# A two-layer encoder on one core: the last MLP products turned to tokens on partitions, and the first products in a written order

## The chip, the cores and the metric

The kernel runs on one core of a Trainium2 chip. A core has TensorE (PE, matrix products), VectorE (DVE), ScalarE (ACT), GpSimd (POOL) and SyncE (SP, which here only starts transfers), each with an instruction stream of its own, and 16 DMA engines. The metric is the device time of one execution in microseconds (us). A weight load of TensorE (PEld in the profile) runs beside the products.

## The reference

A trunk of two layers over x, 512 tokens by 1024 features, float32:

```python
for i in range(2):
    g = sandwich_gains[i]
    h = rms_norm(x, g[0])
    m = parallel_conv_mla(h, ...) if i == 0 else conformer_conv(h, ...)
    x = x + rms_norm(m, g[1])
    h = rms_norm(x, g[2])
    x = x + rms_norm(square(relu(h @ w1[i])) @ w2[i], g[3])      # 1024 -> 4096 -> 1024
return x
```

`parallel_conv_mla` is one combined input projection (1024 to 2208 columns), a gated convolution of width 3 on one part, latent attention with 8 heads on the other, and one output projection. `conformer_conv` is a pointwise product to 2048 columns, a gate, a depthwise convolution of width 31 over the tokens, a LayerNorm, a swish and a second pointwise product. `rms_norm(v, g)` is v times the reciprocal root of its mean square over the 1024 features, times g.

## The kernel before

**Layout.** Everything lies with features on partitions: x is eight tiles of 128 features by 512 tokens. A weight strip is 128 x 1024 (512 KB). `strip` loads one through SP's queue into a raw buffer, ACT casts it to a high part (`whi`, L225), and POOL subtracts that from the raw one for a low part (`wlo`, L226), so that a product of float32 is three products of the shorter type that TensorE takes at full rate: high by high (L248), high by low (L249), low by high (L250). `linear` makes 8 x 3 of them for a strip, into one PSUM bank. Activations are split in the same way (`h`, `hid`): ACT makes the high copy (L232) and DVE the low one (L235).

**Halves.** The tokens are worked in two segments, A and B, of 256 and 256 in layer 0, and of 240 and 272 in layer 1 (A2, B2), since the convolution of half A needs 15 tokens to its right. A written list, M2, names the steps: `('up', 'A', 0, 1, 0, 8)` is half A, layer 0, group 1 of four hidden groups, strips 0 to 8; `down` is the second MLP product, `join` the norm and residual at the end of a sub-layer, `pw1` and `pw2` the pointwise products, `norm` the LayerNorm, `finish` the last norm and the stores. While the chain of one half runs (`join`, `norm`), `pace` and `hold` pull steps of the other half ahead, and `fill` deals out convolution taps between products. The last group of half B's last MLP and its `finish` stand in a list of their own, M3, with nothing beside them; `finish` there gives three of eight tiles to POOL (POOL_OUT) and their stores to ACT's queue.

**Norms.** A mean square is a sum over partitions: squares on ACT (L360), sums of tiles on DVE (L335), then TensorE with a vector of ones (L370) brings one number per token into a column for each 128 tokens. `rstd` (L391 to L428) makes the reciprocal root in some 13 small DVE operations. `spread` brings it back over all partitions by small products with an identity (L435). At the beginning, `R0` is this factor of the first norm, and the evacuations of the first projection's products (L613) multiply by it.

**The start.** `split_x` loads a tile of x, multiplies it by the gain on DVE (L577), and splits it; START lists in which order tiles and the first strips are asked for. Squares of x lag four tiles (LAG). No order is written there: a scheduler places the instructions of all engines by its own model of their times, as in the rest of the program, except for DVE in a part of M2.

Of the kernel before, what the change touches and what calls it, by code (L numbers as in the profile page):

```python
# [35 lines left out]
M2 = [('up', 'A', 0, 0, 0, 8), ('join', 'B', 0, 1), ('down', 'A', 0, 0, 0, 8), ('up', 'A', 0, 1, 0, 8), ('down', 'A', 0, 1, 0, 8), ('up', 'A', 0, 2, 0, 8), ('down', 'A', 0, 2, 0, 8), ('up', 'A', 0, 3, 0, 8), ('down', 'A', 0, 3, 0, 8), ('join', 'A', 0, 3), ('up', 'B', 0, 0, 0, 8), ('down', 'B', 0, 0, 0, 4), ('pw1', 'A', 0, 8), ('down', 'B', 0, 0, 4, 8), ('up', 'B', 0, 1, 0, 8), ('down', 'B', 0, 1, 0, 8), ('up', 'B', 0, 2, 0, 2), ('norm', 'A'), ('up', 'B', 0, 2, 2, 8), ('down', 'B', 0, 2, 0, 8), ('pw2', 'A', 0, 8), ('join', 'A', 1, 1), ('up', 'B', 0, 3, 0, 8), ('down', 'B', 0, 3, 0, 8), ('join', 'B', 0, 3), ('up', 'A', 1, 0, 0, 8), ('down', 'A', 1, 0, 0, 4), ('pw1', 'B', 0, 8), ('down', 'A', 1, 0, 4, 8), ('up', 'A', 1, 1, 0, 8), ('down', 'A', 1, 1, 0, 8), ('up', 'A', 1, 2, 0, 6), ('norm', 'B'), ('up', 'A', 1, 2, 6, 8), ('down', 'A', 1, 2, 0, 8), ('up', 'A', 1, 3, 0, 4), ('pw2', 'B', 0, 8), ('join', 'B', 1, 1), ('up', 'A', 1, 3, 4, 8), ('down', 'A', 1, 3, 0, 8), ('up', 'B', 1, 0, 0, 8), ('down', 'B', 1, 0, 0, 6), ('finish', 'A'), ('down', 'B', 1, 0, 6, 8), ('up', 'B', 1, 1, 0, 8), ('down', 'B', 1, 1, 0, 8), ('up', 'B', 1, 2, 0, 8), ('down', 'B', 1, 2, 0, 8)]  # L36
M3 = [('up', 'B', 1, 3, 0, 8), ('down', 'B', 1, 3, 0, 8), ('finish', 'B')]
# [53 lines left out]
class Seg:  # L91
# [23 lines left out]
HALVES = A, B = Seg(0, T // 2), Seg(T // 2, T)  # L115


A2, B2 = Seg(0, T // 2 - PAD), Seg(T // 2 - PAD, T, PAD)

STARTS = [0, 128, 256, 384, 112, 240, 368]  # L120
# [13 lines left out]
def trunk(ctx: ExitStack, tc: tile.TileContext, a, out: bass.AP):  # L134
# [32 lines left out]
    def accum():  # L167

        scope["turn"] += 1
        tags = [t for t in scope["acc"] if t != "pj" or not (convs or todo or scope.get("chain"))]  # L170
        return ps(tags[scope["turn"] % len(tags)])
# [14 lines left out]
    def ht(dt=F32):  # L186
        return new(ap, "h", 2 * NC, T + PAD, dt=dt)[:, :T]
# [4 lines left out]
    def hpair():  # L192
        return tuple(Win(new(ap, "h", 2 * NC, T + PAD, dt=F32R)) for _ in range(2))
# [6 lines left out]
    vec = cp.tile([P, NV], F32, name="vec")  # L200
    ident = kst[:, K_ID : K_ID + P]
# [70 lines left out]
    late, convs, todo, normed, credit, turn = [], [], [], [], [0.0], [0]  # L272
# [191 lines left out]
    def join(xs, ms, s, post, pre, hs, seg, h, mlp):  # L464
# [4 lines left out]
        hv = views(hs, seg)  # L469
# [101 lines left out]

    s0 = Sum(NC, FULL, nc.gpsimd if ADD0 else nc.vector, whole=W0)

    def split_x(j):
        load_x(xs[j], j)
        t, (hi, lo) = scratch(T), (h.t[:, :T] for h in hs[j])
        nc.vector.tensor_scalar(out=t, in0=xs[j].t, scalar1=col(gains(0, 0) + j), scalar2=None, op0=ALU.mult)  # L577
# [5 lines left out]
    win, j = [], 0  # L583
    for what in START:
        if what == "x":
            split_x(j)
            j += 1
        else:
            win.append(strip(a["win"][len(win)], cuts=what))
    nc.sync.dma_start(kst, a["consts"])  # L590
    nc.sync.dma_start(vec[:, V_QN:], a["vecs"][:, V_QN:])
    settle()
    for j in range(NC - LAG, NC):
        s0.square(xs[j].t)
        settle()
# [12 lines left out]
    def latent(m0, n, gain, slot):  # L608
        lat, ss = [], Sum(n, FULL, whole=WL)
        for j in range(n):  # L610
            acc = linear(win[m0 + j] if m0 + j < len(win) else strip(a["win"][m0 + j]), hs)
            t = tmp("ycat")
            nc.vector.tensor_tensor(out=t, in0=acc, in1=R0, op=ALU.mult)  # L613
# [338 lines left out]
    def finish_step(tok, h):  # L952
        seg = seg_of(h, 1)
        bc = rstds(sums[h], lack.pop(h))
        pool = POOL_OUT[h]
        if pool:
            bcs = tmp("t2")[:, : seg.w]
            nc.scalar.activation(bcs, bc, AF.Copy)

        def add(j, x, m):  # L960
            on_pool = j in pool
            eng = nc.gpsimd if on_pool else nc.vector
            eng.tensor_tensor(out=x, in0=x, in1=m, op=ALU.add)
            queue = nc.scalar if on_pool else nc.sync
            queue.dma_start(out[j * P : (j + 1) * P, seg.sl], x)

        for j in (*pool, *(j for j in range(NC) if j not in pool)):
            on_pool, x, m = j in pool, xs[j][seg.sl], ms[j][seg.sl]
            eng = nc.gpsimd if on_pool else nc.vector
            t = m if on_pool else scratch(seg.w)  # L970
            eng.tensor_tensor(out=t, in0=m, in1=bcs if on_pool else bc, op=ALU.mult)
            settle()
            late.append(lambda j=j, x=x, t=t: add(j, x, t))
            pace(2)
        settle()

    def run(program, in_order=True):
        for tok in program:
# [13 lines left out]
            elif what == "down":  # L992
                need(a["w2"][args[0], args[1], m] for m in range(c0, c1))
                for m in range(c0, c1):
                    add(down_step, h, *args, m)
            elif what == "wout":
# [4 lines left out]
            elif what == "attend":  # L1001
                add(lambda tok, h, half: attend(h, A if half == "A" else B), *args)
# [25 lines left out]
    nc.sync.dma_start(taps, a["taps"])  # L1028
    MLP = dict(acc=["S", "pj", "S", "pj", "S"], hid=("hid", 2 * NC, T), y=("y", 3, T))
# [56 lines left out]
def _pack(i):  # L1086
# [14 lines left out]
    for h in range(H):  # L1101
# [33 lines left out]
        "w2": np.stack([np.stack([_blocks(w2[n, g]) for g in range(4)]) for n in range(2)]),  # L1135
    }
# [18 lines left out]
```

## Time and profile before

| | |
|---|---|
| median of 3 runs | 1166.66 us (1165.98 to 1166.71) |
| the profiled execution | 1166.52 us |
| its span in the profile | 1164.6 us |
| mean granted TensorE clock | 0.996 of full |
| TensorE (PE) busy | 1132.3 us, 97% |
| POOL, ACT, DVE busy | 846.2, 663.8, 645.7 us |
| bytes moved by DMA | 183.99 MB, mean 158 GB/s |

A row of the timeline holds start and duration in us, the engine, the line of the kernel, the operation, output and inputs with their shapes, the number of records (x8) and, in brackets, how long the engine stood idle before and what released it. A row of a group holds the number of instructions, busy time in us, mean ns of one, and the idle time before them. A row of a stretch holds, after its limits: its length, then busy us and number of instructions for PE, PEld, DVE, ACT and POOL, the granted clock, the share of DMA time and GB/s. A product of 512 columns has rows of 0.39 us, which overlap: what counts is the step from one to the next. A row of L370 or L435 in float32 makes two records for each product.

### The profile page before, as it was taken

Reading aid. Unit: us, or ns where it says so; the run is one execution under the profiler, and the core shown is the slowest. Engines: PE = TensorE matmul, PEld = TensorE weight load, DVE = VectorE, ACT = ScalarE, POOL = GpSimd, SP = SyncE. Lnnn points to the kernel's source line nnn. Section 1 sums busy time; section 2 is a strip of 40 time slices with the busy share of each in tenths; the row PEclk is TensorE's granted clock in tenths of the full one; section 3 lists DMA queues with packets and bytes.
Section 4 is the critical chain, followed back from the end, with each engine's and each line's share of the span. In section 5 each row is a group of like instructions: output and inputs, shape, how many; then the busy total and the mean of one; then the engine's idle time right before and its main releaser. Section 6 shows DMA issues by size and latency. Waiting matters only on the chain.

```text
span 1164.6 us, 22863 instructions
## 1 busy us (share of the span) xinstructions
PE 1132.3 (97%) x8850; PEld 1093.1 (94%) x8850; DVE 645.7 (55%) x1696; ACT 663.8 (57%) x1221; POOL 846.2 (73%) x409
## 2 busy tenths in 40 slices
PE   7999989999999999999999999999999999999995
PEld 5788868999999999999999999999999999999995
DVE  5662699554522124499985265599985272322123
ACT  6531677466745457645566778546467685545352
POOL 5663563149988888598886978698887877887681
PEclk9999999999999999999999999999999999999998
DMA  6421332036656555366554555465655554653431
GB/s 209 156 85 30 101 106 73 1 116 231 205 179 198 182 180 187 126 219 195 178 188 161 182 181 191 151 212 192 198 182 181 173 174 161 213 179 123 150 131 39
DMA packets 55405, 183.99 MB, mean 158 GB/s; under 512 B 6401, under 2 KB 10881, under 8 KB 55297
## 3 DMA queue, kind: packets, MB, share of 16 engines
q1 hardware_dynamic: 54720, 181.86, 47.9%
q8 instruction: 69, 1.13, 0.4%
q10 hardware_dynamic: 576, 0.68, 0.2%
q14 instruction: 40, 0.32, 0.1%
HBM read 180.42 MB, written 2.10 MB: 157 GB/s over the span
## 4 chain that ended last, share of the span: by engine, by line
PE 92%; DVE 3%; ACT 3%; DMA 1%; issue 1%; POOL 0%; SPq 0%; POOLq 0%; ACTq 0%
PE S L248 23%; PE S L249 23%; PE S L250 22%; PE pj L248 7%; PE pj L249 7%; PE pj L250 7%; DVE pr L772 1%; PE mi L370 1%; PE mi L435 1%; ACT whi L225 1%; PE mi L775 1%; DVE s L766 1%; PE o L249 1%; PE o L250 0%; DVE pt L238 0%
## 5 line engine op out<-in xcount | busy, mean ns | idle before, releaser
L226 POOL TENSOR_TENSOR wlo<-raw,whi 128x1024 fp32r<-128x1024 f32 (+2 forms) x347 | 802.9, 2335 | 252.2 <-ACT whi L225 243.3
L225 ACT ACTIVATE whi<-raw 128x1024 fp32r<-128x1024 f32 (+2 forms) x347 | 355.7, 1031 | 378.0 <-PE S L249 176.6
L248 PE MATMUL S<-h,whi 128*128 128x256 f32 (+3 forms) x1216 | 346.8, 289 | 6.2 <-ACT h L232 3.4
L250 PE MATMUL S<-h,wlo 128*128 128x256 f32 (+3 forms) x1216 | 349.9, 289 | 0.0
L249 PE MATMUL S<-h,whi 128*128 128x256 f32 (+3 forms) x1216 | 349.8, 289 | 0.1
L248 PEld LDWEIGHTS S<-h,whi 128*128 128x128 f32 x1216 | 227.5, 189 | 12.2 <-ACT h L232 4.2
L249 PEld LDWEIGHTS S<-h,whi 128*128 128x128 f32 x1216 | 229.4, 189 | 4.3 <-DVE h L235 0.5
L250 PEld LDWEIGHTS S<-h,wlo 128*128 128x128 f32 x1216 | 229.5, 189 | 4.0 <-POOL wlo L226 0.3
L248 PE MATMUL S<-hid,whi 128*128 128x256 f32 (+2 forms) x824 | 230.3, 282 | 2.0 <-DVE acc L335 1.8
L249 PE MATMUL S<-hid,whi 128*128 128x256 f32 (+2 forms) x824 | 230.7, 281 | 0.0
L250 PE MATMUL S<-hid,wlo 128*128 128x256 f32 (+2 forms) x824 | 230.0, 280 | 0.0
L837 DVE SCALAR_TENSOR_TENSOR pj<-u,taps,pj 128x240 f32<-128x240 f32 (+1 forms) x464 | 192.4, 481 | 1.3
L248 PEld LDWEIGHTS S<-hid,whi 128*128 128x128 f32 x824 | 154.5, 189 | 2.8 <-DVE acc L335 2.2
L249 PEld LDWEIGHTS S<-hid,whi 128*128 128x128 f32 x824 | 155.4, 189 | 0.2 <-DVE hid L238 0.2
L250 PEld LDWEIGHTS S<-hid,wlo 128*128 128x128 f32 x824 | 155.4, 189 | 0.0
L248 PE MATMUL pj<-h,whi 128*128 128x272 f32 (+3 forms) x336 | 103.6, 308 | 6.9 <-ACT h L232 5.5
L249 PE MATMUL pj<-h,whi 128*128 128x272 f32 (+3 forms) x336 | 103.1, 307 | 0.0
L250 PE MATMUL pj<-h,wlo 128*128 128x272 f32 (+3 forms) x336 | 102.8, 306 | 0.0
L248 PEld LDWEIGHTS pj<-h,whi 128*128 128x128 f32 x336 | 63.7, 190 | 10.1 <-ACT h L232 5.8
L238 DVE TENSOR_TENSOR hid<-S,hid 128x256 fp32r<-128x256 f32 (+2 forms) x103 | 43.1, 419 | 51.2 <-ACT hid L232 50.9
L540 DVE TENSOR_TENSOR m<-S,m 128x256 f32<-128x256 f32 (+2 forms) x74 | 30.6, 416 | 65.3 <-PE S L250 65.3
L249 PEld LDWEIGHTS pj<-h,whi 128*128 128x128 f32 x336 | 63.6, 189 | 3.4 <-DVE h L235 0.9
(247 smaller groups left out, 1683.1 us busy)
## 6 DMA issues: line engine op xcount, KB each, us to landing
raw<-in_w SPq DMA_DIRECT2D x256, 512.0 KB, 3.4
raw<-in_pw SPq DMA_DIRECT2D x48, 512.0 KB, 3.4
raw<-in_win SPq DMA_DIRECT2D x16, 512.0 KB, 3.3
x<-in_xT SPq DMA_DIRECT2D x16, 256.0 KB, 4.2
raw<-in_wout SPq DMA_DIRECT2D x8, 512.0 KB, 3.3
raw<-in_wq SPq DMA_DIRECT2D x8, 192.0 KB, 2.4
out<-x SPq DMA_DIRECT2D x8, 120.0 KB, 2.6
out<-x SPq DMA_DIRECT2D x5, 136.0 KB, 1.7
```

Source lines behind the costliest of these rows:

```text
L225: nc.scalar.activation(h, r, AF.Copy)
L226: nc.gpsimd.tensor_tensor(out=lo[:, c0:c1], in0=r, in1=h.bitcast(F32), op=ALU.subtract)
L238: eng.tensor_tensor(out=lo, in0=src, in1=hi.bitcast(F32), op=ALU.subtract)
L248: nc.tensor.matmul(acc, sh, mh, start=i == 0, stop=False)
L249: nc.tensor.matmul(acc, sh, ml, start=False, stop=False)
L250: nc.tensor.matmul(acc, sl, mh, start=False, stop=i == n - 1)
L370: nc.tensor.matmul(s[:, b : b + 1], q[:, sl.start - self.seg.lo : sl.stop - self.seg.lo], one, start=i == 0, stop=i == len(self.parts) - 1,)
L435: nc.tensor.matmul(o[:, sl], r[:, b : b + 1].to_broadcast([bw, P]), ident[:bw, :bw], start=True, stop=True,)
L540: nc.vector.tensor_tensor(out=m[seg.sl], in0=acc, in1=m[seg.sl], op=ALU.add)
L766: nc.vector.reduce_max(out=mx, in_=S, axis=AX.X)
L772: eng.tensor_scalar(out=pr_, in0=pr_, scalar1=sm, scalar2=None, op0=ALU.mult)
L837: nc.vector.scalar_tensor_tensor(out=dst, in0=src, scalar=wk, in1=acc, op0=ALU.mult, op1=ALU.add)
```

## The change

It has four parts.

- **Segments.** Layer 0 is cut 272 and 240, layer 1 256 and 256. The shift of B2 and `views` go.
- **The last MLP of half B** (`turn`, `residual`, `end` in place of `down` and `finish`): the second products of layer 1 have tokens on partitions. A 128-token block of `hid` is the stationary side and a strip of a second copy of w2 (rows by all 1024 columns) the moving one, 512 columns wide, into four banks (two blocks by two column halves); groups are added up in SBUF. x of half B is turned by 16 transposes on TensorE (`residual_step`). In the last group, `end_step` makes block 0 for all strips, then block 1 in pieces of 512, 256 and 256 columns; each piece is added on DVE, squared on ACT with a sum along the row, and multiplied by the gain on POOL. The reciprocal root is then one number a partition, and the result leaves by DVE and two queues to a second output, `out_b`. M3 and POOL's part of `finish` go. `gtok` is that gain, one row spread over 128 partitions by a transfer on ACT's queue.
- **The start.** Under `manual_schedule` PE, DVE and ACT keep the order in which it is written: nine and three products of zeros (`busy`), and for each tile of x its scale, high copy and rest; the first two strips' products interleaved, tile by tile; then strip 2, and strip 3 around the spread of the first norm.
- **Kept.** The three lines that make `inv0` and `R0` after `spread_sb` are not in the diff, and stand behind the new block, which makes both tiles too.

```diff
-HALVES = A, B = Seg(0, T // 2), Seg(T // 2, T)
-A2, B2 = Seg(0, T // 2 - PAD), Seg(T // 2 - PAD, T, PAD)
+HALVES = A, B = Seg(0, T // 2 + PAD), Seg(T // 2 + PAD, T)
+A2, B2 = Seg(0, T // 2), Seg(T // 2, T)
...
-... ('up', 'B', 1, 0, 0, 8), ('down', 'B', 1, 0, 0, 6), ('finish', 'A'), ('down', 'B', 1, 0, 6, 8), ('up', 'B', 1, 1, 0, 8), ('down', 'B', 1, 1, 0, 8), ('up', 'B', 1, 2, 0, 8), ('down', 'B', 1, 2, 0, 8)]
-M3 = [('up', 'B', 1, 3, 0, 8), ('down', 'B', 1, 3, 0, 8), ('finish', 'B')]
+... ('up', 'B', 1, 0, 0, 8), ('turn', 'B', 1, 0, 0, 6), ('finish', 'A'), ('turn', 'B', 1, 0, 6, 8), ('up', 'B', 1, 1, 0, 8), ('residual', 'B'), ('turn', 'B', 1, 1, 0, 8), ('up', 'B', 1, 2, 0, 8), ('turn', 'B', 1, 2, 0, 8), ('up', 'B', 1, 3, 0, 8), ('end', 'B', 1, 3)]
...
-    def split_x(j):
-        load_x(xs[j], j)
-        t, (hi, lo) = scratch(T), (h.t[:, :T] for h in hs[j])
-        nc.vector.tensor_scalar(out=t, in0=xs[j].t, scalar1=col(gains(0, 0) + j), scalar2=None, op0=ALU.mult)
-        settle()
-        split((hi, lo), t, nc.vector, late=late)
-        if j >= LAG:
-            s0.square(xs[j - LAG].t)
...
+    with tc.manual_schedule(engines={E.PE, E.DVE, E.Activation}):
...
+        scale_x(0)
+        win.append(strip(a["win"][0], cuts=(128,)))
+        rest_x(0)
+        bit(0, 0)
+        busy(3)
+        scale_x(1)
+        win.append(strip(a["win"][1], cuts=(256, 512, 768)))
+        rest_x(1)
+        bit(0, 1)
+        bit(1, 0)
+        bit(1, 1)
+        for j in range(2, NC):
+            scale_x(j)
+            if j >= 4:
+                square_x(j - 4)
+            rest_x(j)
+            bit(0, j)
+            bit(1, j)
+        win.append(strip(a["win"][2]))
...
+        for j in range(1, NC):
+            if j + 3 < NC:
+                square_x(j + 3)
+            if j == 4:
+                win.append(strip(a["win"][3]))
+            last = add_x(j)
+        for k in range(NC):
+            bit(2, k)
+        win.append(strip(a["win"][4]))
+        s0 = Sum(NC, FULL)
+        s0.parts = [last]
+        root = rstd(s0.done(STARTS), D, inverse=inv0)[:, :NB]
+        for k in range(NC - 2):
+            bit(3, k)
+        nc.scalar.activation(R0, spread(root), AF.Copy)
+        for k in range(NC - 2, NC):
+            bit(3, k)
...
+    def turn_mm(acc, h, w, k, b, cols, n):
+        tok = slice(T // 2 + b * P, T // 2 + b * P + P)
+        x, c = hid[h][k], slice(cols.start + n, cols.stop + n)
+        return [
+            (acc[:, cols], x[0][tok], w[0][:, c], k == 0, False),
+            (acc[:, cols], x[0][tok], w[1][:, c], False, False),
+            (acc[:, cols], x[1][tok], w[0][:, c], False, k == NC - 1),
+        ]
...
+        for f in range(2):
+            piece(0, f, slice(0, T))
+        rest(0, slice(0, T))
+        r = root(0)
+        leave(0, r, 1)
+        piece(1, 0, slice(0, T))
+        for i in range(2):
+            cols = slice(i * T // 2, (i + 1) * T // 2)
+            rest(1, cols)
+            piece(1, 1, cols)
+        leave(1, root(1), 2)
...
+    nc.scalar.dma_start(gtok, a["gain"].to_broadcast([P, D]))
```

DVE at the start, before (L577 is the scale, L235 the subtraction for the low part):

```order
L577 TENSOR_SCALAR o_117<-x_80,vec 128x512
L235 TENSOR_TENSOR h_90<-o_117,h_89 128x512
L577 TENSOR_SCALAR mi_137<-x_81,vec 128x512
L577 TENSOR_SCALAR o_142<-x_82,vec 128x512
L577 TENSOR_SCALAR mi_147<-x_83,vec 128x512
L235 TENSOR_TENSOR h_92<-mi_137,h_91 128x512
L235 TENSOR_TENSOR h_94<-o_142,h_93 128x512
L235 TENSOR_TENSOR h_96<-mi_147,h_95 128x512
```

DVE at the start, now (L596 the scale, L602 the subtraction):

```order
L596 TENSOR_SCALAR mi_143<-x_81,vec 128x512
L602 TENSOR_TENSOR h_91<-mi_143,h_90 128x512
L596 TENSOR_SCALAR mi_173<-x_82,vec 128x512
L602 TENSOR_TENSOR h_93<-mi_173,h_92 128x512
L596 TENSOR_SCALAR mi_184<-x_83,vec 128x512
L602 TENSOR_TENSOR h_95<-mi_184,h_94 128x512
L596 TENSOR_SCALAR mi_195<-x_84,vec 128x512
L602 TENSOR_TENSOR h_97<-mi_195,h_96 128x512
```

Three scales stood together ahead of their subtractions; now each subtraction, which needs ACT's copy of its own tile, stands ahead of the next scale.

ACT at the start, before (L225 casts a strip, L232 copies the high part of a tile of x, L360 squares):

```order
L232 ACTIVATE h_93<-o_142 128x512
L232 ACTIVATE h_95<-mi_147 128x512
L360 ACTIVATE mi_158<-x_80 128x512
L360 ACTIVATE mi_166<-x_81 128x512
L232 ACTIVATE h_97<-o_154 128x512
L225 ACTIVATE whi_177<-raw_176 128x1024
L360 ACTIVATE mi_174<-x_82 128x512
```

ACT at the start, now (L220 the cast, L597 the copy, L606 the square):

```order
L597 ACTIVATE h_100<-mi_220 128x512
L606 ACTIVATE ycat_223<-x_82 128x512
L597 ACTIVATE h_102<-mi_233 128x512
L606 ACTIVATE ycat_236<-x_83 128x512
L220 ACTIVATE whi_246<-raw_245 128x1024
L606 ACTIVATE ycat_253<-x_84 128x512
```

The cast of the third strip stood behind the copy of the fifth tile; now it stands behind that of the eighth (`h_102`) and four squares.

PE at the LayerNorm of half A, before (L370 its second sums; the rows go on alike for 34 products to L435, the spread):

```order
L248 MATMUL S_7854<-hid_7260,whi_7683 128x256
L249 MATMUL S_7854<-hid_7261,whi_7683 128x256
L370 MATMUL mi_7795<-kst,acc_7669 128x1 x2
L250 MATMUL S_7854<-hid_7260,wlo_7684 128x256
L248 MATMUL S_7854<-hid_7262,whi_7683 128x256
L249 MATMUL S_7854<-hid_7263,whi_7683 128x256
```

The same place now (L365 the sums, L430 the spread, and then the second pointwise product):

```order
L244 MATMUL S_7943<-hid_7321,whi_7756 128x240
L245 MATMUL S_7943<-hid_7320,wlo_7757 128x240
L365 MATMUL mi_7919<-kst,acc_7793 128x1 x2
L430 MATMUL mi_7969<-kst,s_7923 128x128 x2
L243 MATMUL S_8018<-h_2232,whi_7807 128x256
L243 MATMUL S_8052<-h_2232,whi_7851 128x256
```

The products of half B that stood between sums and spread now stand ahead of both.

PE behind the first spread of the start, now (L365 the second set of sums of the first norm, 10 products ahead of the second L430):

```order
L430 MATMUL mi_349<-kst,s_314 128x128 x4
L585 MATMUL S_330<-h_100,whi_265 128x512
L586 MATMUL S_330<-h_100,wlo_266 128x512
L587 MATMUL S_330<-h_101,whi_265 128x512
L585 MATMUL S_330<-h_102,whi_265 128x512
L586 MATMUL S_330<-h_102,wlo_266 128x512
L587 MATMUL S_330<-h_103,whi_265 128x512
L365 MATMUL mi_364<-kst,ycat_273 128x1 x6
L245 MATMUL S_507<-h_96,wlo_503 128x512
```

Before, the program had one set of sums and one spread, with 28 products of the fourth and fifth strips between them:

```order
L250 MATMUL S_377<-h_99,wlo_373 128x512
L248 MATMUL S_377<-h_101,whi_372 128x512
L249 MATMUL S_377<-h_102,whi_372 128x512
L250 MATMUL S_377<-h_101,wlo_373 128x512
L435 MATMUL mi_225<-kst,s_209 128x128 x4
L248 MATMUL pj_456<-h_87,whi_451 128x512
```

So the second sums and spread are work that was not there.

More of the change, by code (lines that the diff above doesn't have):

```diff
@@ L133, in trunk @@
 @with_exitstack
-def trunk(ctx: ExitStack, tc: tile.TileContext, a, out: bass.AP):
+def trunk(ctx: ExitStack, tc: tile.TileContext, a, out: bass.AP, out_b: bass.AP):
     nc = tc.nc
@@ L169, in accum @@
         scope["turn"] += 1
-        tags = [t for t in scope["acc"] if t != "pj" or not (convs or todo or scope.get("chain"))]
+        tags = [t for t in scope["acc"] if t != "pj" or turned or not (convs or todo or scope.get("chain"))]
         return ps(tags[scope["turn"] % len(tags)])
@@ L179, in scratch @@
         scope["scr"] += 1
-        tags = ["o", "pj", "mi", "pj"] if scope.get("chain") else ["o", "mi"]
+        tags = ["o", "pj", "mi", "pj"] if scope.get("chain") and not turned else ["o", "mi"]
         return ps(tags[scope["scr"] % len(tags)])[:, :w]
@@ L192, in hpair @@
     def hpair():
-        return tuple(Win(new(ap, "h", 2 * NC, T + PAD, dt=F32R)) for _ in range(2))
+        return tuple(Win(new(ap, "h", 2 * NC, dt=F32R)) for _ in range(2))
     def small(w=NB):
@@ L610, in latent @@
         for j in range(n):
[L611 removed]
+            acc = accs[m0 + j] if m0 + j < len(accs) else linear(win[m0 + j], hs)
             t = tmp("ycat")
@@ L930, in pw2_step @@
             sums[h] = Sum(NC, seg, whole=WHOLE[3])
-        acc = linear(take(), views(hs, seg), seg)
+        acc = linear(take(), hs, seg)
         nc.scalar.activation(ms[m][seg.sl], acc, AF.Identity, bias=col(V_BPW2 + m))
@@ L954, in finish_step, with add @@
         bc = rstds(sums[h], lack.pop(h))
[L955 to L971, printed above, removed]
+        def add(j, x, t):
+            nc.vector.tensor_tensor(out=x, in0=x, in1=t, op=ALU.add)
+            nc.sync.dma_start(out[j * P : (j + 1) * P, :], x)
+        for j in range(NC):
+            x, m = xs[j][seg.sl], ms[j][seg.sl]
+            t = scratch(seg.w)
+            nc.vector.tensor_tensor(out=t, in0=m, in1=bc, op=ALU.mult)
             settle()
@@ L975, in finish_step, with banks_step @@
         settle()
+    BLOCKS = [(b, f) for b in range(2) for f in range(2)]
+    def banks_step(h, g):
+        if not turned:
+            for key in BLOCKS:
+                turned[key] = [None, tmp("u")[:, :T], tmp("u")[:, :T]]
+            turned["gain"] = gtok
+        for n, key in enumerate(BLOCKS):
+            turned[key][0] = ps(("S", "pj")[n % 2])
+    def turn_mm(acc, h, w, k, b, cols, n):
[6 more added lines that the diff above has]
+        ]
@@ new lines, in issue, with turn_step @@
+    def issue(lists):
+        for products in zip(*lists):
+            for acc, x, w, start, stop in products:
+                nc.tensor.matmul(acc, x, w, start=start, stop=stop)
+    def turn_step(tok, h, layer, g, k):
+        if k == 0:
+            banks_step(h, g)
+        w = take()
+        for b in range(2):
+            issue([turn_mm(turned[b, f][0], h, w, k, b, slice(0, T), f * T) for f in range(2)])
+        settle()
+        if k == NC - 1:
+            for key in BLOCKS:
+                acc, m, _ = turned[key]
+                if g == 0:
+                    nc.scalar.activation(m, acc, AF.Copy)
+                else:
+                    nc.vector.tensor_tensor(out=m, in0=acc, in1=m, op=ALU.add)
@@ L995, in run @@
                     add(down_step, h, *args, m)
+            elif what == "turn":
+                need(a["w2t"][args[1], k] for k in range(args[2], args[3]))
+                for k in range(args[2], args[3]):
+                    add(turn_step, h, *args[:2], k)
+            elif what == "residual":
+                for b, f in BLOCKS:
+                    add(residual_step, h, b, f)
+            elif what == "end":
+                need(a["w2t"][args[1], k] for k in range(NC))
+                add(end_step, h, *args)
             elif what == "wout":
```

150 lines of the change are left out of this document (107 added, 43 removed).

## The prediction

> **What bounds the kernel now.** I read the page first (span, busy shares, the chain of waits), then stretches of the start, then the timeline where the change cuts, and last the spacing of the products.
>
> ```profile
> span 1164.6 us, 22863 instructions
> ...
> PE 1132.3 (97%) x8850; PEld 1093.1 (94%) x8850; DVE 645.7 (55%) x1696; ACT 663.8 (57%) x1221; POOL 846.2 (73%) x409
> ...
> PE 92%; DVE 3%; ACT 3%; DMA 1%; issue 1%; POOL 0%; SPq 0%; POOLq 0%; ACTq 0%
> ```
>
> TensorE is busy for 97% and holds 92% of the chain, so almost any product added or made wider costs its time. The rest is at the two ends and at a few norms, and those are the places that the change cuts. The profiled execution took 1166.52 us, 0.14 below the median of 1166.66, with 1.9 outside its span; I add my terms to 1166.5.
>
> The start (times from the span's start):
>
> ```profile
> 5.00:10.00 5.00, 3.81 (x7) 1.86 (x8) 2.47 (x4) 3.25 (x7) 2.65 (x3) 1.00 1.00 352
> 10.00:15.00 5.00, 5.00 (x13) 3.79 (x14) 4.90 (x9) 3.88 (x7) 2.54 (x4) 1.00 0.99 347
> ```
> ```profile
> 4.04 0.75 DVE L577 TENSOR_SCALAR mi<-x,vec 128x512 f32<-128x512 f32 x1 [3.17 <-DMA x<-in_xT]
> ...
> 4.83 0.60 ACT L232 ACTIVATE h<-mi 128x512 fp32r<-128x512 f32 x1
> ...
> 5.46 0.69 DVE L235 TENSOR_TENSOR h<-mi,h 128x512 fp32r<-128x512 f32 x1 [0.66 <-ACT h L232]
> ...
> 7.35 0.75 DVE L577 TENSOR_SCALAR o<-x,vec 128x512 f32<-128x512 f32 x1 [1.20 <-DMA x<-in_xT]
> ...
> 12.14 0.68 DVE L235 TENSOR_TENSOR h<-o,h 128x512 fp32r<-128x512 f32 x1
> ...
> 12.74 0.68 DVE L235 TENSOR_TENSOR h<-mi,h 128x512 fp32r<-128x512 f32 x1
> ...
> 13.30 0.63 PE L249 MATMUL pj<-h,whi 128*128 128x512 f32 x1
> ...
> 13.72 0.63 PE L250 MATMUL pj<-h,wlo 128*128 128x512 f32 x1
> ```
> ```profile
> L226 POOL TENSOR_TENSOR wlo<-raw,whi 128x1024 fp32r<-128x1024 f32 x13 | 31.7, 2447 | 16.5 <-ACT whi L225 16.2
> ...
> L360 ACT ACTIVATE mi<-x 128x512 f32<-128x512 f32 x5 | 2.9, 596 | 0.6 <-DVE h L235 0.6
> ```
> ```profile
> 31.88 1.62 PE L370 MATMUL mi<-kst,ycat 128*128 128x1 f32 x14
> ...
> 34.14 0.39 PE L250 MATMUL S<-h,wlo 128*128 128x512 f32 x1
> ...
> 39.69 0.40 PE L250 MATMUL S<-h,wlo 128*128 128x512 f32 x1
> 39.92 1.05 PE L435 MATMUL mi<-kst,s 128*128 128x128 f32 x8
> ...
> 42.39 0.50 PE L248 MATMUL pj<-h,whi 128*128 128x512 f32 x1 [1.41 <-DVE ycat L613]
> ```
>
> Until 10 us the DMA engines are full (352 GB/s) and x comes one tile at a time. From 10 to 15 TensorE is full, but at 0.42 us a product (13.30 to 13.72); from 34.14 to 39.69 it makes 24 steps of 0.231, so the early 0.42 is a clock at about half. By L370, 92 products are done (the 120 of five strips, less the 28 that fit at 0.231 between the end of L370 at 33.4 and the one at 39.69), and at 42.39 TensorE goes on to the sixth strip.
>
> **The change, part by part.**
>
> *The written start.* The DVE now takes x tile by tile: scale, wait for ACT's high copy, subtract, and only then the next scale. From the rows, scale to copy is 0.79 (4.04 to 4.83), copy to subtraction 0.63 (to 5.46), and one DVE instruction to the next 0.60 (12.14 to 12.74): 2.03 a tile with the semaphores. Before, several scales stand together and ACT's copies run behind the next DVE work. The six products of a tile want 6 x 0.231 = 1.39 at full clock, so TensorE waits for DVE and ACT, and zeros that wake its clock can gain nothing there. The second tile lands at 7.35; a broadcast of the last gain, 0.52 MB, now stands first on ACT's queue and at 352 GB/s takes 1.5 of the full DMA time. I take 1.2 of it (ends 0 and 1.5), so the second scale is at 8.55. The eighth high copy ends 6 x 2.03 + 0.79 + 0.60 = 13.57 later. Behind it ACT's written order puts one square (0.60) and then the third strip's cast (1.06, by the row quoted below at the norm); POOL's low part takes 2.45. The third strip's low part is there at 8.55 + 13.57 + 0.60 + 1.06 + 2.45 = 26.2, when 49 products are done. The other 23 of three strips take 5.3: 72 done at 31.6, against 92 before at about the same moment, 20 x 0.231 = 4.6 behind.
>
> *Sums and spread twice.* The lines that make R0 stay behind the new block, which makes it too. So six column sums (1.62 x 12/14 = 1.4), a chain of small DVE operations, four spreads (about 1.0) and a copy are done a second time, and the evacuations wait for the second R0. Between second sums and second spread stand only 10 products, 2.3 us, for a chain of some 2.7 (the last norm's rows, below): 0.4 open. That is 1.4 + 1.0 + 0.4 less what the tail of the first pair saves by running under products (0.6): 2.2. Start together: 4.6 + 2.2 = +6.8, I take **+6.7**. Ends: +2.2, if TensorE loses nothing ahead of the sums, and +8.
>
> *Segments.*
>
> ```profile
> 599.78 0.28 PE L248 MATMUL S<-h,whi 128*128 128x256 f32 x1
> ...
> 605.92 0.28 PE L249 MATMUL S<-h,whi 128*128 128x256 f32 x1
> ```
> ```profile
> 822.18 0.28 PE L248 MATMUL S<-hid,whi 128*128 128x240 f32 x1
> ...
> 825.88 0.27 PE L248 MATMUL S<-hid,whi 128*128 128x240 f32 x1
> ```
> ```profile
> 1059.78 0.29 PE L250 MATMUL S<-h,wlo 128*128 128x272 f32 x1
> ...
> 1066.00 0.29 PE L249 MATMUL S<-h,whi 128*128 128x272 f32 x1
> ```
>
> Steps in these pieces: 52, 33 and 50, so 0.118 for 256 wide, 0.112 for 240, 0.1244 for 272. Layer 0 goes from 256/256 to 272/240: 2112 pairs x (0.1244 + 0.112 - 0.236) = +0.4. Layer 1 goes from 240/272 to 256/256: 960 pairs of MLP-up and pointwise, -0.2; half A's MLP-down, 768 x (0.118 - 0.112) = +4.7. Half B's MLP-down becomes 384 products 512 wide: 384 x 0.231 = 88.7 against 768 x 0.1244 = 95.5, so -6.8. Together **-1.9** (ends -4 and 0, three digits of a pitch over 2000 products).
>
> The Trainium skill (TensorE: Matmul & The Clock Gate, "Back-to-back issue gap") gives about 131 ns for each of a sustained row of 512-wide products; by it the 384 would take 50 us and the sum would be 38 lower. The row says 0.231.
>
> *Residual.* Sixteen transposes on TensorE, 32 records:
>
> ```profile
> 214.43 1.03 PE L775 MATMUL mi<-kst,pr 128*128 128x128 f32 x8
> ```
>
> Spaced (1.03 - 0.27)/7 = 0.109, so **+3.5**, on the full engine (ends 2 and 4.5).
>
> *The norm of half A.*
>
> ```profile
> 625.99 0.50 PE L370 MATMUL mi<-kst,acc 128*128 128x1 f32 x4
> ...
> 627.74 1.06 ACT L225 ACTIVATE whi<-raw 128x1024 fp32r<-128x1024 f32 x1 [2.18 <-PE S L249]
> ...
> 630.41 0.61 PE L435 MATMUL mi<-kst,s 128*128 128x128 f32 x4
> ...
> 632.86 0.49 PE L248 MATMUL S<-h,whi 128*128 128x240 f32 x2 [1.85 <-ACT h L232]
> ```
>
> Between the sums and the spread, 34 products of half B stand before (625.99 to 630.41 holds them) and hide DVE's chain. In the new order sums and spread are neighbours: the wider half's tap chain pulls the products ahead of it. Behind the spread nothing stands but the waiting products, so DVE's chain is open: 2.3 (its 2.8 less the sums' own 0.46). The 1.85 that follows stays.
>
> ```profile
> 1150.74 0.40 ACT L360 ACTIVATE pj<-m 128x272 f32<-128x272 f32 x1 [2.05 <-DVE m L540]
> ...
> 1152.59 0.17 DVE L393 TENSOR_TENSOR mi<-mi,fB 128x3 f32<-128x3 f32 x1 [0.98 <-PE mi L370]
> ...
> 1155.08 0.16 DVE L428 TENSOR_TENSOR s<-mi,fB 128x3 f32<-128x3 f32 x1
> 1155.30 1.65 PE L435 MATMUL mi<-kst,s 128*128 128x128 f32 x6 [2.75 <-DVE s L428]
> ```
> ```profile
> 1150.10 0.14 PE pj L250
> ...
> 1161.09 0.71 POOL x L963
> ```
> ```profile
> L769 ACT ACTIVATION_READ_ACCUMULATOR pr<-S,s 128x1 f32 x32 | 6.3, 196 | 0.0
> ```
>
> At the end of the program a wait of the same kind (2.75 before L435) leaves the spread at 1.65 for 6 records, where 8 took 1.05 at 39.92: the clock had fallen. Two waits of 2.3 and 1.85 close together may do the same, and at the start the products were still at half speed at 13.72, some 4 us after TensorE had become full at 10; 4 us at half clock cost 2.0 (ends 0 and 2.3). **+4.3** for the norm.
>
> The skill (the same page, "What's actually happening") has the clock fall after an idle window of about 3.4 us. By that no wait of 2.3 would cost the 2.0, and the sum would be 1172.4; the end's row, with no wait over 2.75, does not agree.
>
> *The tail.* Before, from the last product's end (1150.10 and 0.14, in the chain's rows) to the end of the span there are 14.3. After it, with tokens on partitions, no sum or spread on TensorE is left: add 0.44 and square 0.40 (the rows at 1150), read the accumulator 0.2 (L769), join the sums 0.2, the chain 2.67 (1152.59 to 1155.24), four adds with a gain of 0.4 = 1.6, and from the last add to the end 2.8 (1161.80 to 1164.6 before): 8.4. So -5.9. POOL's adds go from the path; a strip's order on SP's queue does not matter there, as none is left. But TensorE's last 24 products write the bank which ACT still squares for the half before: add 0.44, square 0.42 and two semaphores, **+1.2**. Tail: **-4.7** (ends -7 and -3).
>
> *Nothing:* the zeros (TensorE waits for the first x anyway); narrower waits at the joins, where a 272-wide chain moves from half B to half A (ends -1.5 and +1.5).
>
> Sum: 6.7 - 1.9 + 3.5 + 4.3 - 4.7 = +7.9, so 1166.5 + 7.9 = **1174**.
>
> **Rivals.** *TensorE, not DVE, is waited for at the start* (no slower). Before, it is full from 10 to 15. If the zeros bring the clock up, the 20 or so products made at 0.42 come at 0.23, which is 4.0 earlier, and the start term is 2.2 - 4.0 = -1.8 in place of +6.7: 1165.9. For it: 5.00 busy of 5.00. Against it: the DVE is at 4.90 in the same stretch. It decides if a tile takes DVE and ACT less than 1.39; the rows add up to 2.03. *The start is worse still*: with TensorE busy two thirds of a cycle its clock stays down until the third strip comes, some 5 us at half cost 2.4, and the gain's transfer holds more tiles than one, 1.5: 1178. *The written start costs nothing* and only the double R0 does: start +2.2, 1170. *The products with 512 columns are far quicker* than 0.231: 38 lower, 1136.
>
> **How the numbers follow.** Start bound by DVE, with the ends of the other terms, the third rival within it: 0.70, from 1169 to 1178. Bound by TensorE: 0.13, about 1166, nearly all of it between 1163 and 1169. Worse start: 0.10, 1178 and above. Quick wide products: 0.01. Tail or spacing gaining some 6 more than the rows give: 0.06, at 1167 to 1169. Within 0.2% (2.3 us, about what a measurement tells from no change) is 1164.3 to 1169: 0.08 of the second and 0.05 of the last, 0.13; faster 0.05 + 0.01 + 0.01 = 0.07; slower 0.80. The range from 1167 to 1178.5 leaves out the second case and half of the worse start.
>
> **What would show it.** In the profile after: scale and subtraction strictly in turn with 2.0 us a tile and TensorE waiting for ACT's copies up to 20 us; the third strip's low part at about 26 us; two groups of six sums; the sixth strip beginning near 49 in place of 42.4; a wait of over 2 us before the spread of half A's norm and doubled products behind it; 32 records of transposes; 512-wide products at 0.231 in the last MLP; and some 8.4 us from the last product to the end. I am wrong if the sixth strip begins before 45, or if the norm's wait is hidden.

## The result and the profile after

The changed kernel takes 1179.45 us (median of 4 runs, 1178.96 to 1181.61) against 1166.68 for the kernel before; the ratio is 1.0113, with an interval of 1.0095 to 1.013. It is slower, as forecast, but by 12.8 us instead of 7.5, and it lies 0.95 above the range.

The page of the changed kernel, span and busy shares, and the chain of waits:

```profile
span 1177.2 us, 22212 instructions
...
PE 1141.9 (97%) x8524; PEld 1086.0 (92%) x8524; DVE 652.2 (55%) x1708; ACT 662.3 (56%) x1212; POOL 846.4 (72%) x408
...
PE 88%; DVE 4%; ACT 4%; DMA 2%; POOL 1%; issue 1%; DVEq 0%; SPq 0%; ACTq 0%; POOLq 0%
```

TensorE is as full as before, at 97% of a span that is 12.6 longer, yet it holds 88% of the chain in place of 92%: other engines now set more of the pace. The timeline of the start:

```profile
6.48 0.75 DVE L596 TENSOR_SCALAR mi<-x,vec 128x512 f32<-128x512 f32 x1 [5.05 <-DMA x<-in_xT]
...
8.50 0.75 DVE L596 TENSOR_SCALAR mi<-x,vec 128x512 f32<-128x512 f32 x1
...
23.62 2.37 POOL L221 TENSOR_TENSOR wlo<-raw,whi 128x1024 fp32r<-128x1024 f32 x1 [9.75 <-ACT whi L220]
...
31.39 1.39 PE L365 MATMUL mi<-kst,ycat 128*128 128x1 f32 x12
...
42.27 1.39 PE L365 MATMUL mi<-kst,ycat 128*128 128x1 f32 x12
...
46.34 1.13 PE L430 MATMUL mi<-kst,s 128*128 128x128 f32 x8 [0.29 <-DVE inv L421]
...
48.94 0.50 PE L243 MATMUL pj<-h,whi 128*128 128x512 f32 x1 [1.47 <-DVE ycat L669]
```

A tile takes DVE 2.02 (6.48 to 8.50), the third strip's low part is there at 26.0, the sums are made twice, and the sixth strip begins at 48.94: 6.55 behind the 42.39 of before. The second spread waits 0.29 for the second root (0.4 was forecast), and behind it TensorE waits another 1.47 for an evacuation.

The norm of half A in the changed kernel, rows of the timeline and then three stretches (the eighth value of a stretch is the granted clock):

```profile
647.84 0.58 PE L365 MATMUL mi<-kst,acc 128*128 128x1 f32 x4 [0.52 <-DVE acc L330]
...
650.74 1.22 PE L430 MATMUL mi<-kst,s 128*128 128x128 f32 x4 [2.32 <-DVE s L416]
653.86 1.01 PE L243 MATMUL S<-h,whi 128*128 128x256 f32 x3 [1.91 <-ACT h L227]
```
```profile
645.00:650.00 5.00, 2.90 (x25) 2.65 (x23) 3.68 (x16) 2.48 (x4) 4.41 (x3) 0.95 0.63 202
650.00:655.00 5.00, 2.36 (x9) 2.06 (x10) 3.13 (x12) 2.55 (x7) 0.77 (x1) 0.50 0.49 177
655.00:660.00 5.00, 5.00 (x27) 5.00 (x27) 3.62 (x11) 3.88 (x10) 0.00 (x0) 0.53 0.00 0
```

Between the sums and the spread nothing runs on TensorE for 2.3, and behind the spread it waits 1.9 more. The clock falls in the first of the two waits: the 0.95 up to 650 is some 0.5 us at half speed (0.05 x 5 / 0.5), and the spread at 650.74 already takes 1.22 for its four records, against 0.61 in the kernel before (630.41). It stays at half until about 659.7 (the 0.53 is 4.7 of 5 us at half), some 10 us in all. The Trainium skill (TensorE: Matmul & The Clock Gate, "What's actually happening") has the clock fall after an idle window of about 3.4 us; no single wait here is that long, so the row speaks against reading it as one unbroken gap. What TensorE's rows show is that of the 3.4 us before the fall, with the sums among them, it was busy for about half.

A wait that the prediction did not have stands at the end of attention, ahead of the first output product (W_out) of half A:

```profile
231.53 0.38 PE L243 MATMUL o<-pt,h 128*128 128x256 f32 x1 [0.69 <-ACT pt L227]
...
232.25 0.39 PE L244 MATMUL o<-pt,h 128*128 128x256 f32 x1 [0.34 <-DVE pt L233]
...
233.85 0.38 ACT L227 ACTIVATE ycat<-o 64x256 fp32r<-64x256 f32 x1 [2.38 <-PE o L245]
...
234.28 0.40 PE L243 MATMUL S<-ycat,whi 128*128 128x272 f32 x1 [0.47 <-ACT ycat L227]
```

Attention is still cut at token 256, while the output product of half A is 272 wide, so it needs the last head of both halves. Before, a half's output products needed the heads of that half alone, and TensorE's list of waits from 214 to 230 was empty.

The tail in the changed kernel:

```profile
1167.86 0.28 PE L1051 MATMUL pj<-whi,hid 128*128 128x256 f32 x1
1168.24 0.42 DVE L1090 TENSOR_TENSOR u<-pj,u 128x256 f32<-128x256 f32 x1 [3.83 <-PE pj L1051]
1168.70 0.39 ACT L1092 ACTIVATE pj<-u 128x256 f32<-128x256 f32 x1 [3.75 <-DVE u L1090]
...
1169.25 0.79 DVE L1100 SCALAR_TENSOR_TENSOR mi<-s,s,s 128x1 f32<-128x1 f32 x1 [0.58 <-ACT pj L1092]
...
1172.79 1.67 DVE L1112 SCALAR_TENSOR_TENSOR u<-u,s,u 128x256 f32<-128x256 f32 x4
```

From the last product's end (1168.1) to the span's end (1177.2) there are 9.1, in place of 14.4.

### The profile page after: what moved, and what is told of

Its sections match the earlier page's. It is cut to its first block, busy times and chain, and to the rows that moved or that the text cites. A ratio compares the mean times of both kernels' runs of the same rounds, so it can differ in the third digit from the quotient of the medians.

```text
span 1177.2 us, 22212 instructions
## 1 busy us (share of the span) xinstructions
PE 1141.9 (97%) x8524; PEld 1086.0 (92%) x8524; DVE 652.2 (55%) x1708; ACT 662.3 (56%) x1212; POOL 846.4 (72%) x408
## 4 chain that ended last, share of the span: by engine, by line
PE 88%; DVE 4%; ACT 4%; DMA 2%; POOL 1%; issue 1%; DVEq 0%; SPq 0%; ACTq 0%; POOLq 0%
PE S L243 20%; PE S L244 20%; PE S L245 20%; PE pj L243 5%; PE pj L244 5%; PE pj L245 5%; PE pj L1051 4%; PE S L1051 4%; ACT whi L220 1%; DVE pr L828 1%; POOL wlo L221 1%; DMA raw<-in_win 1%; PE mi L430 1%; PE mi L365 1%; PE mi L831 1%
## 5 line engine op out<-in xcount | busy, mean ns | idle before, releaser
L220 ACT ACTIVATE whi<-raw 128x1024 fp32r<-128x1024 f32 (+2 forms) x347 | 356.3, 1033 | 365.3 <-PE S L244 169.6
L243 PE MATMUL S<-h,whi 128*128 128x256 f32 (+3 forms) x1192 | 340.5, 289 | 5.0 <-ACT h L227 2.9
L245 PE MATMUL S<-h,wlo 128*128 128x256 f32 (+3 forms) x1192 | 342.4, 288 | 0.0
L244 PE MATMUL S<-h,whi 128*128 128x256 f32 (+3 forms) x1192 | 342.3, 288 | 0.0
L893 DVE SCALAR_TENSOR_TENSOR pj<-u,taps,pj 128x256 f32<-128x256 f32 x464 | 192.6, 483 | 1.3
L243 PE MATMUL S<-hid,whi 128*128 128x256 f32 (+2 forms) x664 | 185.5, 281 | 1.4 <-DVE acc L330 1.2
L244 PE MATMUL S<-hid,whi 128*128 128x256 f32 (+2 forms) x664 | 186.4, 281 | 0.0
L245 PE MATMUL S<-hid,wlo 128*128 128x256 f32 (+2 forms) x664 | 186.4, 282 | 0.0
L243 PEld LDWEIGHTS S<-hid,whi 128*128 128x128 f32 x664 | 124.8, 189 | 2.5 <-DVE acc L330 1.9
L245 PEld LDWEIGHTS S<-hid,wlo 128*128 128x128 f32 x664 | 125.4, 189 | 0.0
L244 PEld LDWEIGHTS S<-hid,whi 128*128 128x128 f32 x664 | 125.2, 189 | 0.0
L243 PE MATMUL pj<-h,whi 128*128 128x256 f32 (+3 forms) x328 | 98.7, 301 | 1.9 <-DVE ycat L669 1.5
L245 PE MATMUL pj<-h,wlo 128*128 128x256 f32 (+3 forms) x328 | 98.9, 302 | 0.0
L244 PE MATMUL pj<-h,whi 128*128 128x256 f32 (+3 forms) x328 | 98.3, 300 | 0.0
L245 PEld LDWEIGHTS pj<-h,wlo 128*128 128x128 f32 x328 | 62.3, 190 | 2.1 <-issue 0.2
```

Of the source, the lines that this page charges most:

```text
L220: nc.scalar.activation(h, r, AF.Copy)
L243: nc.tensor.matmul(acc, sh, mh, start=i == 0, stop=False)
L244: nc.tensor.matmul(acc, sh, ml, start=False, stop=False)
L245: nc.tensor.matmul(acc, sl, mh, start=False, stop=i == n - 1)
L893: nc.vector.scalar_tensor_tensor(out=dst, in0=src, scalar=wk, in1=acc, op0=ALU.mult, op1=ALU.add)
```

## The experiments

All times below are against runs of the kernel before on the same chip in the same session.

**The former start in the changed kernel.**

```diff
-    with tc.manual_schedule(engines={E.PE, E.DVE, E.Activation}):
...
+    def split_x(j):
...
+    win, j = [], 0
+    for what in START:
...
```

START, LAG and the single R0 are again as in the kernel before.

> The changed kernel with the former start (split_x, no zeros, one R0); the gain's transfer stays first on ACT's queue. Theory 1 (the loss is made of separate pieces: the written start, an uncovered norm, wider segments): the sixth strip begins at 43 to 45 in place of 48.9, and the whole takes 1173 to 1175 us, 5 to 6.5 less than the changed kernel. Theory 2 (what the start loses is slack that later waits hide, and the loss lies in the spacing of the products): within 1 of the changed kernel, 1178.5 or more.

1174.6 us, ratio 1.0058 [1.0045, 1.0071]: the loss at the start is not hidden later, so theory 2 fell. The sixth strip begins at

```profile
43.93 0.50 PE L246 MATMUL pj<-h,whi 128*128 128x512 f32 x1 [1.98 <-DVE ycat L609]
```

5.0 earlier than in the changed kernel. What remains against 42.39 comes from the gain's transfer: the next kernel has the same start without it, and begins the strip at 42.51. (The profiled executions differ by 4.5 in span, 1177.2 against 1172.7.)

**The segments alone in the kernel before.**

```diff
-HALVES = A, B = Seg(0, T // 2), Seg(T // 2, T)
-A2, B2 = Seg(0, T // 2 - PAD), Seg(T // 2 - PAD, T, PAD)
+HALVES = A, B = Seg(0, T // 2 + PAD), Seg(T // 2 + PAD, T)
+A2, B2 = Seg(0, T // 2), Seg(T // 2, T)
...
-        return tuple(Win(new(ap, "h", 2 * NC, T + PAD, dt=F32R)) for _ in range(2))
+        return tuple(Win(new(ap, "h", 2 * NC, dt=F32R)) for _ in range(2))
...
-            attend(h, A if half == "A" else B)
+            attend(h, A2 if half == "A" else B2)
```

> The kernel before with the new segments alone (272/240, then 256/256), former start and former last MLP. Theory 1: the norm of half A loses its cover (+6: wait and clock), the first output product of half A waits for the other half's last head (+2), layer 0's pairs cost +3, layer 1's pairs 0.2396 against 0.2378 (+3.8): 1180 to 1182 us. Theory 2 (the 0.1198 of 256-wide products in layer 1 comes with the turned products' strips or with the run, not with the segments): layer 1's 256-wide products at 0.118, and 1173 to 1176.

1178.35 us, ratio 1.0091 [1.0078, 1.0103]: the segments alone lose most of what the whole change loses, though the amount of work is the same. Neither theory had the time: theory 1's sum is 1.7 too high at its lower end. In its trace the products of layer 1 that read h are at 0.1200, so theory 2 fell (no turned strip is in this kernel). The stretch from the first spread of the latent norms to the first sums of half A's join is 3.1 longer than before (117.46 to 244.06, against 116.91 to 240.36), about 1.8 of it in waits and the rest in the wider output products, and the waits at half A's norm are there. That the 0.1200 comes from the cut itself, as theory 1 had it, fell with wide_h below: this kernel also has the narrower tiles of h.

**One R0.**

```diff
...
-    R0 = cp.tile([P, T], F32, name="R0")
-    inv0 = cp.tile([P, len(STARTS)], F32, name="inv0")
-    nc.scalar.activation(R0, spread(rstd(s0.done(STARTS), D, inverse=inv0)[:, :NB]), AF.Copy)
```

> The changed kernel without the second sums, root, spread and copy of R0. Theory 1: the sixth strip begins at 46.4 to 47.0 in place of 48.9, the whole -2 to -2.5, some 1177.2 us. Theory 2 (evacuations are late anyway, since the third strip's cast sets the start): no change beyond 0.5.

1174.12 us, ratio 1.0058 [1.0046, 1.0071], more than either theory had. In its trace TensorE goes from the spread to the sixth strip with products all the way:

```profile
40.35 1.05 PE L430 MATMUL mi<-kst,s 128*128 128x128 f32 x8
...
44.91 0.39 PE L243 MATMUL pj<-h,whi 128*128 128x512 f32 x1
```

At the sixth strip the second R0 costs 4.0 and not 2.2: besides its own 2.4 of sums and spread, it makes the evacuations wait, and TensorE with them. Its removal also shows what the written order by itself costs there: 44.91 against 43.93 for the former start with the same transfer, 1.0. That does not last: at the first spread of the latent norms the two are level (118.32 and 118.24; the changed kernel is at 122.49), and so are their times. The whole gains more than 4 in this pair of profiles, 5.6 in span, since the clock also stays at half for a shorter time at half A's norm (6.8 in place of 10.2).

**Cover for the norm of half A.**

```diff
-('pw2', 'A', 0, 8), ('join', 'A', 1, 1), ('up', 'B', 0, 3, 0, 8)
+('up', 'B', 0, 3, 0, 2), ('pw2', 'A', 0, 8), ('join', 'A', 1, 1), ('up', 'B', 0, 3, 2, 8)
```

> The changed kernel with two steps of half B (two up strips of group 3) placed ahead of pw2 of half A, so that 24 products stand between the second sums and the spread of the LayerNorm of half A. Theory 1: the wait of 2.3 goes and the clock stays up: -4 to -6, 1173.5 to 1175.5 us. Rival: the clock falls for another reason (the 1.9 wait behind the spread is enough): only -2.3, 1177. Second rival: the join of half A in layer 1 lacks the two steps, and gets the wait: no change.

1177.19 us, ratio 1.0081 [1.0067, 1.0094]: some 3.7 less than the changed kernel by the two ratios, and above theory 1's range. 24 products now stand between sums and spread, and the clock holds up to 660:

```profile
650.00:655.00 5.00, 5.00 (x47) 5.00 (x46) 2.02 (x10) 3.04 (x5) 4.52 (x3) 1.00 0.59 202
655.00:660.00 5.00, 2.56 (x21) 2.21 (x20) 3.15 (x13) 3.97 (x10) 4.26 (x2) 1.00 0.57 210
660.00:665.00 5.00, 5.00 (x27) 4.81 (x28) 4.09 (x13) 4.71 (x13) 0.00 (x0) 0.66 0.31 108
```

The wait behind the spread stays, and in this execution the clock still falls behind it: 0.66 over 5 us is half speed for 3.4 of them. So the first rival is partly right: the one remaining wait can be enough. It need not be: in the profile of the five repairs below the same wait, 2.4 long, leaves the clock at 1.00.

**The tiles of h 528 columns apart.**

```diff
-        return new(ap, "h", 2 * NC, dt=dt)
+        return new(ap, "h", 2 * NC, T + PAD, dt=dt)[:, :T]
...
-        return tuple(Win(new(ap, "h", 2 * NC, dt=F32R)) for _ in range(2))
+        return tuple(Win(new(ap, "h", 2 * NC, T + PAD, dt=F32R)) for _ in range(2))
```

> The changed kernel with the tiles of h again 528 columns apart in memory (512 used), as in the kernel before; nothing else. Layout theory (the spacing of products hangs on where the operands lie): layer 1's 256-wide products return from 0.1200 to 0.118 and the early 512-wide ones from 0.227 to 0.231, together some 2900 x 0.002 - 650 x 0.004 = 3 to 5 us less, 1175 to 1177. Rival (the spacing comes from the columns of the segments or from the mix of work): 0.1200 and 0.227 stay, no change.

1177.16 us, ratio 1.0089 [1.0077, 1.0101], against 1.0113 [1.0095, 1.013]: less, but the intervals overlap, so the time alone does not decide. The spacing of the products, from the timeline of the changed kernel:

```profile
35.69 0.39 PE L586 MATMUL S<-h,wlo 128*128 128x512 f32 x1
...
38.41 0.39 PE L244 MATMUL S<-h,whi 128*128 128x512 f32 x1
...
862.65 0.28 PE L244 MATMUL S<-h,whi 128*128 128x256 f32 x1
...
865.89 0.28 PE L244 MATMUL S<-h,whi 128*128 128x256 f32 x1
```

and from that with the wider tiles:

```profile
35.75 0.39 PE L585 MATMUL S<-h,whi 128*128 128x512 f32 x1
...
38.52 0.39 PE L243 MATMUL S<-h,whi 128*128 128x512 f32 x1
...
862.59 0.28 PE L243 MATMUL S<-h,whi 128*128 128x256 f32 x1
...
865.91 0.28 PE L244 MATMUL S<-h,whi 128*128 128x256 f32 x1
```

These are 12, 27, 12 and 28 steps: 0.2267 and 0.1200 in the changed kernel, 0.2308 and 0.1186 with wider tiles. The layout theory holds: the same products on the same columns are spaced otherwise when their tiles lie otherwise. It is the place of h that counts: averaged over both traces at full clock, the 256-wide products that read h step 0.1199 and 0.1180, while those that read hid step 0.1186 and 0.1185. Why the place of a tile costs time, these runs don't tell.

**The gain's transfer later.**

```diff
-    nc.scalar.dma_start(gtok, a["gain"].to_broadcast([P, D]))
+    nc.sync.dma_start(gtok, a["gain"].to_broadcast([P, D]))
```

> The changed kernel with the gain's 0.5 MB on SP's queue behind the first strips and tiles of x. Theory: the first scale starts at 4.1 in place of 6.5; the second tile of x then sets the pace (7.4 to 7.8), and all that follows comes 1 to 1.5 us earlier: 1178. Rival: the DMA engines are full until 15 either way, and the last tile of x lands no sooner: no change.

1180.1 us, ratio 1.0115 [1.01, 1.013]: no change. The first scale comes at 4.04 and the second, which sets the pace, at 8.22 instead of 8.50 (the first sums at 31.20 instead of 31.39):

```profile
4.04 0.75 DVE L596 TENSOR_SCALAR mi<-x,vec 128x512 f32<-128x512 f32 x1 [2.61 <-DMA x<-in_xT]
...
8.22 0.76 DVE L596 TENSOR_SCALAR mi<-x,vec 128x512 f32<-128x512 f32 x1 [2.06 <-DMA x<-in_xT]
```

The rival's outcome is right: in this written order, a late first tile costs nothing that the second tile's landing does not cost anyway.

**No zeros.**

```diff
-        busy(9)
...
-        busy(3)
```

> The changed kernel without the 12 products of zeros. Theory (DVE and ACT set the start, 2.02 a tile): the first products run at half clock, six of them take 2.56 a tile, so TensorE itself falls behind for some tiles, but the third strip's low part still comes at 26 and TensorE has caught up by then: within 1 us. Rival (the clock sets the start): 2 to 4 us slower, 1181.5 to 1183.5.

1180.59 us, ratio 1.0114 [1.0101, 1.0127], against 1.0113 with the zeros: they are worth nothing that these runs show, though with these intervals an effect of 2 us could hide. The profiled execution begins the sixth strip at 50.96, 2.0 later than the changed kernel's, chiefly because the clock is at half from 26.5 to 29.9 (granted 0.50). That is not the missing zeros: the profile of norm_cover2, which has them, shows the same fall and the same 50.96. The rival in which the clock sets the start finds no support; 2 us of it are not excluded by the times alone.

**Five repairs together.** One R0, the gain late, the cover, a bank (S) of its own for the last 256 columns, and in the start:

```diff
+        scale_x(2)
         rest_x(1)
...
-            scale_x(j)
+            if j + 1 < NC:
+                scale_x(j + 1)
+            if j == 4:
+                win.append(strip(a["win"][2]))
...
-        win.append(strip(a["win"][2]))
```

> The changed kernel with five repairs: one R0; the gain's transfer on SP's queue behind x; in the written start each scale ahead of the former tile's subtraction, and the third strip's cast ahead of the squares; two steps of half B as cover for the LayerNorm of half A; and the last 256 columns in a bank of their own. Theory: sixth strip at 40.5 to 42.5 in place of 48.9 (-6.5 to -8.5), norm -3.5, last wait -1.1: 1166.5 to 1169 us, equal to the kernel before or up to 2 slower. Rival (gains at the start come back as later waits): 1172 or more.

1165.29 us, ratio 0.9985 [0.9975, 0.9996], 1.2 below the theory's range: the gains at the start do not come back as waits. The third strip's low part is there at 19.0 (26.0 before the repair), the sixth strip begins at 41.73, and the start's stretches are full:

```profile
15.00:20.00 5.00, 5.00 (x23) 4.08 (x23) 4.55 (x8) 5.00 (x10) 2.40 (x1) 0.98 0.40 161
20.00:25.00 5.00, 5.00 (x24) 4.14 (x23) 4.16 (x6) 3.54 (x6) 2.33 (x1) 1.00 0.31 105
```

Of the 14.4 by which the two profiles differ in span, 7.6 lie ahead of the first spread of the latent norms (114.92 against 122.49), 5.3 at half A's norm, where the clock does not fall in this execution, and 1.3 at the bank. The repairs inside the written start were not run one by one.

**The same with the wider tiles**, and **the repaired start alone in the kernel before**:

> best1 with the tiles of h 528 columns apart. If the spacing that the run of wide_h showed (0.118 and 0.231) adds to the five repairs: some 2.5 to 3 less than best1, 1162 to 1163 us. If the wider tiles help only where waits are open: equal to best1, 1165.

> The kernel before with the repaired written start alone (one R0, scales ahead of subtractions, the third strip's cast ahead of the squares, zeros in front); segments and last MLP as before. Theory (the order of the start, not the writing of it, was at fault): 868 half-products done at 114.9 in place of 116.9, the whole 1165 to 1166. Rival (the scheduler's own start was as good; best1 gained elsewhere): 1167 or more.

The first takes 1163.77 us, ratio 0.9963 [0.995, 0.9977], and is the fastest kernel here, some 4 us below the one before. The wider tiles add to the repairs: 2.2 thousandths below the five repairs by the two ratios, 2.4 in wide_h. The second takes 1168.72, ratio 1.0006 [0.9997, 1.0015]: the repaired start is no better than the scheduler's own, and its rival is right. Its sums come at 28.2 in place of 31.9, but with 72 products done in place of 92, and the sixth strip begins at 41.91, only 0.5 before the 42.39. Then TensorE waits behind the next root and rotation, by the list of waits from 40 to 120:

```profile
PE mi L370 <- DVE s L421: 0.8, 1, 0.8
PE mi L729 <- DVE ycat L727: 0.5, 1, 0.5
```

At the first spread of the latent norms it is at 118.02, against 116.91 in the kernel before and the 114.9 of its theory.

So what best1w gains on the kernel before does not come from the start. Two of the runs above bear on the turned products: the changed kernel with the former start (1174.6) and the segments alone (1178.35) differ in the turned last MLP with its tail and in the gain's transfer, and the one with them is 3.8 us faster, with intervals that do not meet. That the whole gain of best1w lies there, after the price of the segments, no run of its own shows.

## Why the prediction was wrong in size

The two profiled executions differ by 12.6 in span, the forecast sum was 7.9. The measured column is worked out from the two traces: a step from one product to the next is compared with the mean step of products of the same width and source at full clock, and what it takes beyond that is counted as waiting (the clock's fall included).

| term | forecast | measured |
|---|---|---|
| start, up to the sixth strip | +6.7 | +6.55 |
| waits at the end of attention | none | +2.2 |
| norm of half A | +4.3 | +6.1 |
| other waits at joins | 0 | -2.1 |
| residual | +3.5 | +1.7 |
| spacing of products behind the start | -1.9 | +2.1 |
| tail, with the shared bank | -4.7 | -4.0 |

The step that failed most is the spacing of the products under the new segments, 4.0 off; the waits at attention's end (2.2) had no term at all, and the norm was 1.8 too small. The residual and the other joins made up for 3.9 of these by luck.

- **Segments: the missed step.** Two things were wrong in this term. First, the 0.1244 for 272 columns came from one piece whose products read h. Those that read hid are slower, by a piece of the kernel before:

```profile
980.35 0.29 PE L248 MATMUL S<-hid,whi 128*128 128x272 f32 x1
...
982.61 0.29 PE L248 MATMUL S<-hid,whi 128*128 128x272 f32 x1
```

These are 18 steps of 0.1256. So layer 0 costs some 2.8 and not 0.4 (its own figures, 2112 x 0.0004, already give 0.8). Second, the change also narrows h's tiles from 528 to 512 columns, in a line that I let go as nothing. With it layer 1's products that read h cost 3.1 more in place of 0.2 less, and the early 512-wide ones some 1.3 less. wide_h puts this line at 2.4 thousandths of the time, some 2.8 us, the steps of the two traces at 1.8 behind the start; without it the term would be near 0 and still not -1.9. No row of before showed the line's cost, and the term should have had a wider end above.
- **Start: right sum, wrong parts, so the sum is luck.** The cycle of 2.03 a tile (2.02) and the third strip's low part at 26.2 (26.0) came as worked out, and the sums came at 31.4 with 72 products done. But the step from the 20 missing products to a lasting 4.6 failed: the kernel before stands still for its spread and first evacuation (2.47 from L435 to the sixth strip), and the new order puts that under products. The written order and the transfer together cost 2.5 at the sixth strip (44.91 against 42.39), and the order's share of it is gone by 118 (one_r0 and old_start). The second R0 costs 4.0, which I put at 2.2 because my sum had no wait of TensorE for the late evacuations.
- **Attention: not looked at.** The order shows that W_out of half A stands behind the last head; I looked at waits only where the diff touched steps. No run repairs this one, so its 2.2 rest on the traces of the changed kernel and of seg_only.
- **Norm: right mechanism, too small.** The open wait is 2.3 as forecast; the clock stayed at half for some 10 us rather than 4. In the profiles of six other runs with the same two waits (old_start, seg_only, one_r0, wide_h, gain_late, no_zeros) it was 6.8, so part of the excess belongs to this execution. The cover brings back 3.7 of 6.1.
- **Residual: mis-sized.** A transpose makes one record and not two: 16 records spaced 0.109, 1.7.
- **Tail.** 9.1 from last product to end in place of 8.4: joining the three sums took 0.79 (L1100) and not 0.2. The shared bank cost a wait of 1.1 at 1165.0, 1.2 by forecast (it is gone in best1).
- **Rivals.** TensorE waited for at the start is out: the cycle of a tile is 2.02 and not under 1.39, and no_zeros shows no loss. "The written start costs nothing and only the double R0 does" comes nearest to one_r0 and old_start, with 4.0 for the R0 in place of 2.2. The worse start did partly come about: in the executions of norm_cover2 and no_zeros, the clock is at half for 3.4 us between 25 and 30, in the wait for the third strip, and the sixth strip begins at 50.96.

## What to carry to other kernels

A start written by hand is worth what its slowest alternation is worth: write down one cycle of each engine in the written order, and put the next tile's independent work ahead of the instruction that waits. Then compare it with the scheduler's own order, which was as good here. When halves of the work cover each other's chains, moving the cut by a few columns moves every cover: look in the new order at what stands between each sum and its spread, not only where steps change. A line that changes only a tile's width in memory is an edit of its own, and wants a run of its own.

## What was not expected of the hardware

- The spacing of products follows the place of the tiles they read: 256 columns at 0.1200 with h's tiles 512 columns apart and 0.1186 with 528; 512 columns the other way round, 0.2267 and 0.2308. Products that read hid stayed as they were.
- In the changed kernel's profile TensorE's clock fell to half inside a wait of 2.3, before the wait of 1.9 behind it, and stayed there for some 10 us (0.50 and 0.53); with the same two waits it was 6.8 us in six other runs. After a single wait of about 2 it fell for 3.4 us in some executions (0.66 over 5 us) and not in others.
- The clock column can read 1.00 where the products step as if at half: from 10 to 15 in the kernel before they step at 0.42 against 0.231 later, a ratio of 1.8. At half A's norm in the changed kernel, where the column reads 0.53, 256-wide products step at 0.213 against 0.120, the same ratio.
- Twelve products of zeros changed nothing that these runs show, where another engine's chain of 2.02 a tile sets the pace.
